# A planned decoder kernel: the DeltaNet inverse from 32-wide blocks, and two changes to the plan of its start

## The chip, the cores and the metric

One core of one Trainium2 chip runs the whole kernel. The metric is the device time in microseconds (us) of one execution, as the median of several runs. A profiled execution gives the trace; its span goes from the first instruction to the last.

## What is computed

Two decoder layers over 256 tokens of width 1024, float32. Each layer projects the normalised input once, runs three mixers side by side (gated DeltaNet, pooling, sparse attention with 64 keys a query), and merges them through gates and two projections. The part that matters here is DeltaNet, cut from the reference, with 4 heads and chunks of 64 tokens:

```
lmat = where(strict, (k_beta @ k^T) * decay, 0)      # 64 x 64, strictly lower
tmat = triangular_solve(eye + lmat, eye)             # unit lower triangular inverse
u    = tmat @ v_beta
w    = tmat @ (k_beta * exp(gc))
# per chunk: v_new = u - w @ state; o = q*exp(g) @ state + attn @ v_new; state = ...
```

The kernel works with chunks of 128 tokens, two of them, so it inverts eight 128 x 128 triangular matrices a layer (2 chunks, 4 heads).

## The kernel before

**The plan.** The code does not issue instructions in its own order. Each call on V, S, G, PE or DMA (VectorE, ScalarE, GpSimd, TensorE, and SyncE's DMA queue) is recorded as an operation with a modelled cost, and a planner (class Plan, lines 186 to 546) lays all of them out in time and then emits one fixed order for each engine. `cost` (line 222 on) holds the modelled costs; `lay_out` (line 353 on) is the list scheduler. TensorE takes operations by their place in the code plus a shift; the other engines take them by how late they may be, a due time that `deadlines` works back from the layout before. Six layouts are made and the best one by the model is kept. All instructions appear in the trace under line 544, where they are emitted, so the rows are read by tile names.

Buffers come from tags with a fixed number of slots, handed out in the order of the code. The mx banks (4 PSUM banks) may be handed out of order, but at most 6 places ahead of the first one not yet handed out (WM, line 60). Weights come in as raw (5 slots), are cast to a high part wh (mostly by ScalarE) and a low part wl (a VectorE subtraction of 128 x 1024), and each product with the 1024-wide input is made of three full-tile matmuls into a pj bank.

**Planned landing of DMAs.** Lines 513 to 515 add to a model of the transfers 600 ns and DELAY (line 52), 900 ns, for each DMA:

```python
dma_free = max(dma_free, at + (2500.0 if e == "POOL" else 1360.0)) + o.tail
o.end = dma_free + 600.0 + DELAY
```

The tail of a DMA is its bytes by 120, 262, 318 or 338 a ns, by the length of its rows (line 229). SyncE's queue starts at 730 ns in the model.

**Parameter rows.** Lines 643 to 648 load the conv weights, pool scales and output norm of both layers as 106 rows through GpSimd's DMA queue. Lines 697 to 704 turn them with one TensorE transpose into pt (128 x 2 x 53), copied out by ScalarE, and make hb, half of five columns, on VectorE. This stands before the first projection in the code, so its mx bank is the second one in the order (the first is that of the 40 warming matmuls). Its first user is the conv of the k columns (`wc` in the loop over qkv), far later.

**The inverse** (lines 1161 to 1189). Um holds the negated, scaled, strictly upper part of each matrix; uc holds its eight sets of 32 x 32 diagonal blocks side by side, 128 x 8 x 32. Before the change the two 16 x 16 halves of each diagonal block are inverted together, on VectorE, in 15 steps from r = 15 down to 1. A step has three VectorE operations on 8 x (16 - r) elements of each partition, each waiting for the one before it:

```python
V.stream_shuffle(xb[:, :, r:], x16[:, :, r:], [r] * 16 + [16 + r] * 16)
V.tensor_tensor(xb[:, :, r:], xb[:, :, r:], u16[:, :, r:r + 1].to_broadcast([128, 8, n]), op=ALU.mult)
V.tensor_tensor(x16[:, :, r:], x16[:, :, r:], xb[:, :, r:], op=ALU.add)
```

The halves are then put on the diagonal of xi, a VectorE transpose makes xt, and `joined` (line 1181) is called twice: 32 matmuls of 32 x 32 each (8 matrices, 4 row bands, the bands inside), um times xt and that times xi, which fills the off-diagonal quarter.

**From 32 to 128** (lines 1217 to 1256). For both chunks: p1, eight 32 x 32 matmuls; p2, four matmuls for tt's 32..64 rows (copied there by VectorE) and eight more; then p3, two times four matmuls of 64 x 64, with copies between them. The results Qm feed the DeltaNet recurrence (`four`), whose output o0, o1 is normalised, multiplied by the projected gate (`gated`), transposed into yah and yal, and multiplied into the branch projection, the third of the layer's three. The gate projections and the branch projections of the other two mixers do not depend on it.

A float32 matmul of TensorE shows as two records in the trace, one of a 4-byte split (fp32r) as one.

Of the kernel before, what the change touches and what calls it, by code (L numbers as in the profile page):

```python
# [9 lines left out]
F32 = mybir.dt.float32  # L10
# [20 lines left out]
for _n, _c in (("ident", 128), ("upper", 128), ("supper", 128), ("bd", 128),  # L31
               ("ncaus", 128), ("eye16", 16), ("cosa", 128), ("sina", 128), ("cosi", 64),
               ("sini", 64), ("rcount", 64), ("half", 2), ("strict", 128)):
    CST[_n] = (_w, _w + _c)
    _w += _c
# [10 lines left out]
SWITCH = 160.0  # L46
# [5 lines left out]
DELAY = 900.0  # L52
# [12 lines left out]
def constants():  # L65
# [13 lines left out]
    put("eye16", (p % 16) == np.arange(16)[None, :])  # L79
    put("half", np.concatenate([p % 32 < 16, p % 32 >= 16], axis=1))  # L80
# [105 lines left out]
class Plan:  # L186
# [35 lines left out]
    def cost(self, eng, call, args, kw):  # L222
# [8 lines left out]
        if eng == "PE":  # L231
            if call == "transpose":
                return 109.0, 170.0, False
            if args[1].ap.dtype == F32R:
                return (n / 2.4 + 13.3 if n > 100 else 60.0), 175.0, False
            m, k = args[1].shape[-1], args[1].shape[0]
            if k <= 32:
                return 12.0, 170.0, False
            if k <= 64:
                return 116.0, 170.0, False  # L240
            return 2 * (max(n, m) / 1.2 + 3), 170.0, False
# [111 lines left out]
    def lay_out(self):  # L353
# [98 lines left out]
        while len(order) < len(self.ops):  # L452
# [60 lines left out]
            if o.call == "dma_start":  # L513
                dma_free = max(dma_free, at + (2500.0 if e == "POOL" else 1360.0)) + o.tail
                o.end = dma_free + 600.0 + DELAY
# [33 lines left out]
def trunk(ctx: ExitStack, tc: tile.TileContext, x, norm_g, w_in, gate_b, conv_w, a_log, dt_bias, dn_onorm,  # L549
# [126 lines left out]
    um = make("um", [128, 8, 32])  # L676
    G.memset(um, 0.0)

# [16 lines left out]


    plan.shift = LATE + 300
    pp = bank("mx")
    PE.transpose(pp[:, :DEPTH * NPAR], rows[:DEPTH * NPAR, :], ident[:DEPTH * NPAR, :DEPTH * NPAR])
    pts = make("pt", [128, DEPTH, NPAR], F32)  # L700
    S.copy(pts, pp[:, :DEPTH * NPAR].rearrange("p (l n) -> p l n", l=DEPTH))
    hbs = make("hb", [128, DEPTH, 5], F32)
    V.tensor_scalar(hbs, pts[:, :, 48:53], 0.5, None, op0=ALU.mult)
    plan.shift = 0
# [17 lines left out]
    for l in range(DEPTH):  # L722
# [57 lines left out]
        pt, hb = pts[:, l], hbs[:, l]  # L780
# [139 lines left out]
        attend("q", QC)  # L920
        attend("v", VC)
# [238 lines left out]

        lower, upper_ = con("half")[:, 1:2], con("half")[:, 0:1]
        w16 = unit()
        u16, x16, xb = (w16[:, i * 128:(i + 1) * 128].rearrange("p (n j) -> p n j", n=8) for i in range(3))
        V.scalar_tensor_tensor(u16, uc[:, :, 16:], lower, uc[:, :, :16], op0=ALU.mult, op1=ALU.add)
        V.tensor_scalar(um[:, :, 16:], uc[:, :, 16:], upper_, None, op0=ALU.mult)
        V.tensor_copy(x16, con("eye16")[:, None, :].to_broadcast([128, 8, 16]))
        for r in range(15, 0, -1):
            n = 16 - r
            V.stream_shuffle(xb[:, :, r:], x16[:, :, r:], [r] * 16 + [16 + r] * 16)
            V.tensor_tensor(xb[:, :, r:], xb[:, :, r:], u16[:, :, r:r + 1].to_broadcast([128, 8, n]), op=ALU.mult)  # L1170
            V.tensor_tensor(x16[:, :, r:], x16[:, :, r:], xb[:, :, r:], op=ALU.add)

        xi = make("xi", [128, 8, 32], F32)
        w32 = unit()
        xt, z32 = (w32[:, i * 256:(i + 1) * 256].rearrange("p (n j) -> p n j", n=8) for i in range(2))
        V.tensor_scalar(xi[:, :, :16], x16, upper_, None, op0=ALU.mult)
        V.tensor_scalar(xi[:, :, 16:], x16, lower, None, op0=ALU.mult)
        V.transpose(xt, xi)
        bands = [slice(32 * b, 32 * b + 32) for b in range(4)]

        def joined(lhs, rhs):
            ps = bank("mx")[:, :256].rearrange("p (n j) -> p n j", n=8)
            for i in range(8):
                for bs in bands:
                    mm(ps[bs, i], lhs[bs, i], rhs[bs, i], True, True)
            return ps

        S.copy(z32, joined(um, xt))
        V.tensor_tensor(xi, joined(z32, xi), xi, op=ALU.add)

# [31 lines left out]
        pairs = [(a, slice(64 * a, 64 * a + 32), slice(64 * a + 32, 64 * a + 64)) for a in range(2)]  # L1222
        for c in range(2):
            c4 = slice(4 * c, 4 * c + 4)
            p1 = bank("mx")[:, :256].rearrange("p (a h j) -> p a h j", a=2, h=4)
            for a, lo32, hi32 in pairs:
                for h in range(4):
                    mm(p1[hi32, a, h], v4(Um[c])[lo32, h, hi32], tt[lo32, 4 * c + h, 0:32], True, True)
                (S.copy if a else V.tensor_copy)(y1[hi32, a, c4], p1[hi32, a])
        Qm = []  # L1230
        for c in range(2):
# [8 lines left out]
            p2 = bank("mx")[:, :384].rearrange("p (a h j) -> p a h j", a=3, h=4)  # L1240
            for h in range(4):
                mm(p2[32:64, 2, h], xi[32:64, 4 * c + h], y1[32:64, 0, 4 * c + h], True, True)
            V.tensor_copy(tt[32:64, c4, 0:32], p2[32:64, 2])
            for a, lo32, hi32 in pairs:
                for h in range(4):
                    mm(p2[lo32, a, h], y1[hi32, a, 4 * c + h], xi[hi32, 4 * c + h], True, True)
# [167 lines left out]
```

## Time and profile before

| | |
|---|---|
| median of 3 runs | 575.1 us (574.57 to 575.27) |
| profiled execution | 574.95 us, of which its span is 573.2 us |
| TensorE matmuls | 565.2 us busy, 99% of the span |
| TensorE weight loads | 497.9 us, beside the matmuls |
| VectorE | 482.7 us, 84% |
| ScalarE | 297.8 us, 52% |
| GpSimd | 40.3 us, 7% |
| granted TensorE clock | 1.00 in every stretch |
| DMA | 98.7 MB, 56.7% of 16 engines' span on the main queue |

How to read it: the busy share says which engine is full, not which one sets the end; for that the waits and the timeline are read. A busy time counts an instruction from its start to its end, and neighbours overlap: so what an operation takes out of a full engine's stream is the distance from one start to the next. In a timeline row the first number is the start and the second the time that the merged instructions cover, both in us. In a windows row each engine has its busy time in the stretch and the number of instructions, then come the granted clock, the DMA share and GB/s.

### The profile page before, as it was taken

How to read it: one execution, taken by the hardware profiler on the slowest of the kernel's cores; microseconds unless marked ns; L12 is line 12 of the kernel's file. 1: busy time of each engine (PE TensorE's matmuls, PEld its weight loads, DVE VectorE, ACT ScalarE, POOL GpSimd, SP SyncE). 2: the span in 40 equal slices, each digit the busy share in tenths (PEclk: the TensorE clock that was granted, in tenths of full speed). 3: DMA queues.
4: the chain of work that ended last, by engine and by line, in shares of the span. 5: the costliest groups of instructions: out<-in, count | busy, mean ns of one | idle time of the engine just before them, and what ended most of it. 6: DMA issues, size and time to landing. Idle time of an engine off the chain costs nothing. (4 is left out here: it accounts for less than half of the span.)

```text
span 573.2 us, 10046 instructions
## 1 busy us (share of the span) xinstructions
PE 565.2 (99%) x3750; PEld 497.9 (87%) x3750; DVE 482.7 (84%) x1026; ACT 297.8 (52%) x572; POOL 40.3 (7%) x49
## 2 busy tenths in 40 slices
PE   8999999999999999999999999999999999999997
PEld 7787999999888788888879889999998878888886
DVE  5995999999999767758599999999999966785672
ACT  6654646656563443644366645756454534444520
POOL 4210020000000101000011002000000020100000
PEclk9999999999999999999999999999999999999999
DMA  8795548283686543664646459457456643657411
GB/s 285 233 283 151 140 114 224 64 231 131 227 255 203 181 132 109 216 220 151 182 126 198 122 145 244 111 148 210 136 186 205 203 157 89 200 168 238 161 38 73
DMA packets 89792, 98.70 MB, mean 172 GB/s; under 512 B 5616, under 2 KB 58656, under 8 KB 89744
## 3 DMA queue, kind: packets, MB, share of 16 engines
q1 hardware_dynamic: 89184, 97.47, 56.7%
q0 software_dynamic: 560, 0.60, 0.6%
q8 instruction: 29, 0.48, 0.3%
q14 instruction: 19, 0.16, 0.1%
HBM read 97.00 MB, written 1.05 MB: 171 GB/s over the span
## 5 line engine op out<-in xcount | busy, mean ns | idle before, releaser
L544 ACT CAST wh<-raw 128x1024 fp32r<-128x1024 f32 (+2 forms) x167 | 175.0, 1052 | 158.5 <-PE pj L544 116.0
L544 DVE TENSOR_TENSOR wl<-raw,wh 128x1024 fp32r<-128x1024 f32 (+1 forms) x174 | 209.6, 1217 | 18.0 <-PE pj L544 10.7
L544 PE MATMUL pj<-wh,hh 128*128 128x512 f32 (+1 forms) x352 | 101.3, 389 | 0.4 <-ACT hh L544 0.4
L544 PE MATMUL pj<-wl,hh 128*128 128x512 f32 (+1 forms) x352 | 101.2, 387 | 0.0
L544 PE MATMUL pj<-wh,hl 128*128 128x512 f32 (+1 forms) x352 | 99.7, 386 | 0.4 <-DVE hl L544 0.3
L544 PEld LDWEIGHTS pj<-wh,hl 128*128 128x128 f32 x352 | 65.1, 188 | 14.1 <-DVE hl L544 1.9
L544 PEld LDWEIGHTS pj<-wh,hh 128*128 128x128 f32 x352 | 64.5, 188 | 12.9 <-ACT hh L544 1.3
L544 PEld LDWEIGHTS pj<-wl,hh 128*128 128x128 f32 x352 | 64.8, 188 | 12.0
L544 PE MATMUL pj<-hh,wh 128*128 128x256 f32 x384 | 56.3, 285 | 0.0
L544 PE MATMUL pj<-hh,wl 128*128 128x256 f32 x384 | 54.9, 284 | 0.0
L544 PE MATMUL pj<-hl,wh 128*128 128x256 f32 x384 | 54.6, 284 | 0.0
L544 PE MATMUL pj<-wh,y 128*128 128x512 f32 (+1 forms) x208 | 51.6, 383 | 0.0
L544 PEld LDWEIGHTS pj<-hh,wh 128*128 128x128 f32 x384 | 50.4, 191 | 0.2
L544 PEld LDWEIGHTS pj<-hh,wl 128*128 128x128 f32 x384 | 49.8, 192 | 0.0
L544 PEld LDWEIGHTS pj<-hl,wh 128*128 128x128 f32 x384 | 49.7, 192 | 0.0
L544 PEld LDWEIGHTS pj<-wh,y 128*128 128x128 f32 x208 | 38.5, 188 | 7.5
L544 PE MATMUL mx<-wh,y 128*128 128x512 f32 (+1 forms) x128 | 38.4, 380 | 0.0
L544 PEld LDWEIGHTS mx<-u,u 128*128 128x128 f32 (+2 forms) x336 | 31.3, 164 | 3.2 <-issue 1.4
L544 PE MATMUL mx<-u,u 128*128 128x128 f32 (+2 forms) x336 | 32.9, 249 | 0.0
L544 DVE SCALAR_TENSOR_TENSOR u<-pj,pt,u 128x255 f32<-128x255 f32 (+2 forms) x72 | 29.3, 470 | 0.0
L544 PE MATMUL pj<-wl,y 128*128 128x512 f32 (+1 forms) x104 | 29.2, 387 | 0.0
L544 PEld LDWEIGHTS mx<-wh,y 128*128 128x128 f32 x128 | 23.3, 188 | 4.4 <-DVE y L544 0.2
(210 smaller groups left out, 662.5 us busy)
## 6 DMA issues: line engine op xcount, KB each, us to landing
raw<-in_w_in_dram SPq DMA_DIRECT2D x128, 512.0 KB, 4.0
raw<-in_w_branch_dram SPq DMA_DIRECT2D x24, 512.0 KB, 4.0
raw<-in_w_out_dram SPq DMA_DIRECT2D x16, 512.0 KB, 3.2
tg<-in_gate_b_dram SPq DMA_DIRECT2D x12, 256.0 KB, 4.2
raw<-in_w_in_dram SPq DMA_DIRECT2D x4, 486.0 KB, 6.5
x_sb<-in_x_dram SPq DMA_DIRECT2D x2, 512.0 KB, 4.4
out_dram<-x_sb SPq DMA_DIRECT2D x3, 256.0 KB, 2.0
raw<-in_w_in_dram SPq DMA_DIRECT2D x2, 324.0 KB, 5.1
```

The source lines that it names most:

```text
L544: getattr(self.real[o.eng], o.call)(*[put(a) for a in o.args], **{k: put(v) for k, v in o.kw.items()})
```

## The change

The inverse of a 32 x 32 diagonal block is made in one piece: 31 steps on VectorE from r = 31 to 1, on 8 x (32 - r) elements each; the 16-wide halves, um, the two joining products and the constants for them go. p1 and p2 have their loops over the two 64-row halves inside the loop over heads; the four extra matmuls of p2 go, and VectorE transposes p2's first result instead of copying the extra one. The parameter rows are turned after the attention's q heads of layer 0 instead of before the first projection. In the planner, the 900 ns are added only to DMAs issued after 10 us, a switch between small and full tiles costs 103 ns instead of 160, and matmuls of up to 32 and 64 rows cost 21 and 134 ns instead of 12 and 116. The diff, with the constants' renaming left out:

```diff
-SWITCH = 160.0
+SWITCH = 103.0
-DELAY = 900.0
+DELAY, CALM = 900.0, 10000.0
...
             if k <= 32:
-                return 12.0, 170.0, False
+                return 21.0, 170.0, False
             if k <= 64:
-                return 116.0, 170.0, False
+                return 134.0, 170.0, False
...
-                o.end = dma_free + 600.0 + DELAY
+                o.end = dma_free + 600.0 + (DELAY if at > CALM else 0.0)
...
-    um = make("um", [128, 8, 32])
-    G.memset(um, 0.0)
...
-    plan.shift = LATE + 300
-    pp = bank("mx")
-    PE.transpose(pp[:, :DEPTH * NPAR], rows[:DEPTH * NPAR, :], ident[:DEPTH * NPAR, :DEPTH * NPAR])
-    pts = make("pt", [128, DEPTH, NPAR], F32)
-    S.copy(pts, pp[:, :DEPTH * NPAR].rearrange("p (l n) -> p l n", l=DEPTH))
-    hbs = make("hb", [128, DEPTH, 5], F32)
-    V.tensor_scalar(hbs, pts[:, :, 48:53], 0.5, None, op0=ALU.mult)
-    plan.shift = 0
...
         attend("q", QC)
+        if l == 0:
+
+            pp = bank("mx")
...
+        pt, hb = pts[:, l], hbs[:, l]
         attend("v", VC)
...
-        V.scalar_tensor_tensor(u16, uc[:, :, 16:], lower, uc[:, :, :16], op0=ALU.mult, op1=ALU.add)
-        V.tensor_scalar(um[:, :, 16:], uc[:, :, 16:], upper_, None, op0=ALU.mult)
-        V.tensor_copy(x16, con("eye16")[:, None, :].to_broadcast([128, 8, 16]))
-        for r in range(15, 0, -1):
...
-        V.tensor_scalar(xi[:, :, :16], x16, upper_, None, op0=ALU.mult)
-        V.tensor_scalar(xi[:, :, 16:], x16, lower, None, op0=ALU.mult)
-        V.transpose(xt, xi)
...
-        S.copy(z32, joined(um, xt))
-        V.tensor_tensor(xi, joined(z32, xi), xi, op=ALU.add)
+        xb = make("xb", [128, 8, 32], F32)
+        V.tensor_copy(xi, con("eye32")[:, None, :].to_broadcast([128, 8, 32]))
+        for r in range(31, 0, -1):
+            n = 32 - r
+            V.stream_shuffle(xb[:, :, r:], xi[:, :, r:], [r] * 32)
+            V.tensor_tensor(xb[:, :, r:], xb[:, :, r:], uc[:, :, r:r + 1].to_broadcast([128, 8, n]), op=ALU.mult)
+            V.tensor_tensor(xi[:, :, r:], xi[:, :, r:], xb[:, :, r:], op=ALU.add)
...
+            for h in range(4):
+                for a, lo32, hi32 in pairs:
+                    mm(p1[hi32, a, h], v4(Um[c])[lo32, h, hi32], tt[lo32, 4 * c + h, 0:32], True, True)
             for a, lo32, hi32 in pairs:
-                for h in range(4):
-                    mm(p1[hi32, a, h], v4(Um[c])[lo32, h, hi32], tt[lo32, 4 * c + h, 0:32], True, True)
                 (S.copy if a else V.tensor_copy)(y1[hi32, a, c4], p1[hi32, a])
...
             for h in range(4):
-                mm(p2[32:64, 2, h], xi[32:64, 4 * c + h], y1[32:64, 0, 4 * c + h], True, True)
-            V.tensor_copy(tt[32:64, c4, 0:32], p2[32:64, 2])
+                for a, lo32, hi32 in pairs:
+                    mm(p2[lo32, a, h], y1[hi32, a, 4 * c + h], xi[hi32, 4 * c + h], True, True)
+            V.transpose(tt[32:64, c4, 0:32], p2[0:32, 0])
             for a, lo32, hi32 in pairs:
-                for h in range(4):
-                    mm(p2[lo32, a, h], y1[hi32, a, 4 * c + h], xi[hi32, 4 * c + h], True, True)
                 S.copy(q4[lo32, :, hi32], p2[lo32, a])
```

## Rows read from the trace of the kernel before

**Rows 1.** The page's busy times: us, share of the span, instructions.

```profile
PE 565.2 (99%) x3750; PEld 497.9 (87%) x3750; DVE 482.7 (84%) x1026; ACT 297.8 (52%) x572; POOL 40.3 (7%) x49
```

**Rows 2.** TensorE's waits: for whom, total us, times, longest us.

```profile
PE mx L544 <- DVE big L544: 1.6, 4, 0.9
...
PE mx L544 <- ACT kiT L544: 0.9, 1, 0.9
```

**Rows 3.** Timeline of TensorE, 189 to 202 us, around layer 0's inverse.

```profile
189.15 1.07 PE L544 MATMUL pj<-wl,hh 128*128 128x512 f32 x4
190.15 0.75 PE L544 MATMUL mx<-u,um 32*32 32x32 f32 x64
190.83 1.20 PE L544 MATMUL pj<-wh,hh 128*128 128x512 f32 x4
191.87 1.08 PE L544 MATMUL pj<-wh,hl 128*128 128x512 f32 x4
...
197.19 0.89 PE L544 MATMUL mx<-u,u 32*32 32x32 f32 x32
198.01 0.50 PE L544 MATMUL pj<-wl,hh 128*128 128x512 f32 x1
...
200.73 0.34 PE L544 MATMUL mx<-u,xi 32*32 32x32 f32 x5
...
201.86 0.73 PE L544 MATMUL pj<-wl,hh 128*128 128x512 f32 x2
```

**Rows 4.** Timeline of VectorE: the inverse and its end in both layers.

```profile
163.32 0.19 DVE L544 STREAM_SHUFFLE u<-u 128x8 f32<-128x8 f32 x1
...
176.04 0.22 DVE L544 STREAM_SHUFFLE u<-u 128x64 f32<-128x64 f32 x1
...
176.82 0.26 DVE L544 STREAM_SHUFFLE u<-u 128x72 f32<-128x72 f32 x1
...
184.22 0.29 DVE L544 STREAM_SHUFFLE u<-u 128x104 f32<-128x104 f32 x1
...
185.16 0.29 DVE L544 STREAM_SHUFFLE u<-u 128x112 f32<-128x112 f32 x1
...
188.57 0.47 DVE L544 TENSOR_SCALAR xi<-u,cs 128x128 f32<-128x128 f32 x2
...
194.36 0.42 DVE L544 TENSOR_TENSOR xi<-mx,xi 128x256 f32<-128x256 f32 x1 [2.12 <-PE mx L544]
...
238.38 0.75 DVE L544 SCALAR_TENSOR_TENSOR y<-mx,hb,y 128x512 fp32r<-128x512 f32 x1 [0.62 <-ACT y L544]
...
459.52 0.42 DVE L544 TENSOR_TENSOR xi<-mx,xi 128x256 f32<-128x256 f32 x1 [1.82 <-PE mx L544]
```

**Rows 5.** Groups of instructions of VectorE: busy us, mean ns of one, idle before.

```profile
L544 DVE STREAM_TRANSPOSE u<-xi 128x256 f32<-128x256 f32 x4 | 1.7, 436 | 0.0
```

**Rows 6.** Busy time of each engine in three stretches.

```profile
40.00:60.00 20.00, 19.14 (x97) 15.98 (x96) 14.22 (x32) 11.73 (x28) 0.00 (x0) 1.00 0.59 162
60.00:160.00 100.00, 99.72 (x772) 96.13 (x772) 99.81 (x228) 59.63 (x120) 5.82 (x5) 1.00 0.57 165
189.00:216.00 27.00, 27.00 (x350) 22.09 (x349) 18.09 (x31) 12.10 (x25) 3.65 (x2) 1.00 0.53 162
```

**Rows 7.** Timeline of TensorE: the first matmuls of DeltaNet's branch projection, both layers.

```profile
255.85 1.98 PE L544 MATMUL pj<-wh,y 128*128 128x512 f32 x8
...
534.62 1.98 PE L544 MATMUL pj<-wh,y 128*128 128x512 f32 x8
```

**Rows 8.** The parameter rows' transpose in the timeline, and the first use of its result.

```profile
53.34 0.25 PE L544 MATMUL mx<-cs,rows 106*128 106x106 f32 x1
...
L544 ACT ACTIVATE u<-pj,pt x24: 452/468/498, 97.0 to 393.5; 128x256 f32<-128x256 f32 x24
```

**Rows 9.** Timeline of VectorE at the start: first readers of x and of a weight.

```profile
4.13 0.69 DVE L544 SCALAR_TENSOR_TENSOR f<-x_sb 128x512 f32<-128x512 f32 x1 [3.27 <-DMA x_sb<-in_x_dram]
...
8.69 0.70 DVE L544 CAST wh<-raw 128x1024 fp32r<-128x1024 f32 x1 [0.23 <-DMA raw<-in_w_in_dram]
```

More of the change, by code (lines that the diff above doesn't have):

```diff
@@ L31 @@
 for _n, _c in (("ident", 128), ("upper", 128), ("supper", 128), ("bd", 128),
-               ("ncaus", 128), ("eye16", 16), ("cosa", 128), ("sina", 128), ("cosi", 64),
-               ("sini", 64), ("rcount", 64), ("half", 2), ("strict", 128)):
+               ("ncaus", 128), ("eye32", 32), ("cosa", 128), ("sina", 128), ("cosi", 64),
+               ("sini", 64), ("rcount", 64), ("strict", 128)):
     CST[_n] = (_w, _w + _c)
@@ L78, in constants @@
     put("ncaus", np.where(j > p, FILL, 0.0))
-    put("eye16", (p % 16) == np.arange(16)[None, :])
-    put("half", np.concatenate([p % 32 < 16, p % 32 >= 16], axis=1))
+    put("eye32", (p % 32) == np.arange(32)[None, :])
     for n, dim in (("a", 128), ("i", 64)):
@@ L920, in trunk @@
         attend("q", QC)
+        if l == 0:
+            pp = bank("mx")
+            PE.transpose(pp[:, :DEPTH * NPAR], rows[:DEPTH * NPAR, :], ident[:DEPTH * NPAR, :DEPTH * NPAR])
+            pts = make("pt", [128, DEPTH, NPAR], F32)
+            S.copy(pts, pp[:, :DEPTH * NPAR].rearrange("p (l n) -> p l n", l=DEPTH))
+            hbs = make("hb", [128, DEPTH, 5], F32)
+            V.tensor_scalar(hbs, pts[:, :, 48:53], 0.5, None, op0=ALU.mult)
+        pt, hb = pts[:, l], hbs[:, l]
         attend("v", VC)
@@ L1157, in trunk @@
         V.tensor_scalar(c1, eg[:, 4:8], -1.0, None, op0=ALU.mult)
-        lower, upper_ = con("half")[:, 1:2], con("half")[:, 0:1]
-        w16 = unit()
-        u16, x16, xb = (w16[:, i * 128:(i + 1) * 128].rearrange("p (n j) -> p n j", n=8) for i in range(3))
-        V.scalar_tensor_tensor(u16, uc[:, :, 16:], lower, uc[:, :, :16], op0=ALU.mult, op1=ALU.add)
-        V.tensor_scalar(um[:, :, 16:], uc[:, :, 16:], upper_, None, op0=ALU.mult)
-        V.tensor_copy(x16, con("eye16")[:, None, :].to_broadcast([128, 8, 16]))
-        for r in range(15, 0, -1):
[L1168 to L1171, printed above, removed]
-        xi = make("xi", [128, 8, 32], F32)
-        w32 = unit()
-        xt, z32 = (w32[:, i * 256:(i + 1) * 256].rearrange("p (n j) -> p n j", n=8) for i in range(2))
-        V.tensor_scalar(xi[:, :, :16], x16, upper_, None, op0=ALU.mult)
-        V.tensor_scalar(xi[:, :, 16:], x16, lower, None, op0=ALU.mult)
-        V.transpose(xt, xi)
[L1179 to L1186, printed above, removed]
-        S.copy(z32, joined(um, xt))
-        V.tensor_tensor(xi, joined(z32, xi), xi, op=ALU.add)
+        xi = make("xi", [128, 8, 32], F32)
+        xb = make("xb", [128, 8, 32], F32)
[5 more added lines that the diff above has]
+            V.tensor_tensor(xi[:, :, r:], xi[:, :, r:], xb[:, :, r:], op=ALU.add)
         for c in range(2):
@@ L1239, in trunk @@
                             .to_broadcast([128, 4, 4, 32]), op=ALU.mult)
-            p2 = bank("mx")[:, :384].rearrange("p (a h j) -> p a h j", a=3, h=4)
+            p2 = bank("mx")[:, :256].rearrange("p (a h j) -> p a h j", a=2, h=4)
             for h in range(4):
-                mm(p2[32:64, 2, h], xi[32:64, 4 * c + h], y1[32:64, 0, 4 * c + h], True, True)
-            V.tensor_copy(tt[32:64, c4, 0:32], p2[32:64, 2])
+                for a, lo32, hi32 in pairs:
+                    mm(p2[lo32, a, h], y1[hi32, a, 4 * c + h], xi[hi32, 4 * c + h], True, True)
+            V.transpose(tt[32:64, c4, 0:32], p2[0:32, 0])
             for a, lo32, hi32 in pairs:
-                for h in range(4):
-                    mm(p2[lo32, a, h], y1[hi32, a, 4 * c + h], xi[hi32, 4 * c + h], True, True)
                 S.copy(q4[lo32, :, hi32], p2[lo32, a])
```

1 line of the change is left out of this document (removed).

## The prediction

> **What bounds the kernel now.** I read the busy shares first: TensorE's matmuls cover 565.2 of 573.2 us, VectorE's work 482.7 [rows 1]. So the end is set by how much TensorE has to do and by the little that it waits. Next the waits of TensorE: the two longest kinds are four waits for big, 1.6 us together, and one for kiT, 0.9 us [rows 2]; three more kinds are shorter. Then TensorE's timeline where the DeltaNet inverse is made, to see what each small group takes out of the stream [rows 3]; then VectorE's timeline, to see what the inverse takes there [rows 4]; last, the room between the inverse and the matmuls that cannot start without it [rows 6, 7]. What to see: an operation that leaves TensorE is worth its place in the stream, and VectorE work is free only as long as its result comes before TensorE has used up everything else.
>
> **Removed from TensorE: the two joining products.** Each is 32 matmuls, 64 records. Four full-tile matmuls take 0.91 us in the stream, so after the four that start at 189.15 the next was due at 190.06; it came at 190.83, and those four took 1.04 instead of 0.91 [rows 3]. One group costs 0.77 + 0.13 = 0.90 us, its entry and exit included; the other three groups of the two layers look alike in the timeline. Four times 0.90 is **3.6 us**.
>
> **The small products that stay.** The first group (p1) has 32 records in 0.82 us, 25.6 ns each; the second (p2) 48 records in 1.13 us, 23.5 ns each [rows 3]. In both, most neighbours use the same 32x32 tile of the array. In the joining product each neighbour uses another of four tiles: 64 records in 0.68 us, 10.6 ns each. The change alternates two tiles in p1 and p2, and p2 loses its four extra matmuls of each chunk (48 records become 32). Bounds for 32 records: 0.34 us at 10.6 ns, 0.82 us at 25.6 ns. I take half of the one-tile rate, since only two tiles alternate: 0.41 us each. p1 saves 0.41 (0 to 0.48), p2 0.72 (0.31 to 0.79), 1.13 a layer, **2.3 us** for both (0.6 to 2.5). The 64-wide products of p3 keep their order and price.
>
> TensorE in all: 3.6 + 2.3 = **5.9 us less** (4.2 to 6.1).
>
> **The transpose by VectorE** takes the place of a VectorE copy of the same columns. The nearest row, a transpose of twice the columns, is 0.44 us [rows 5]. There are four, in the same place of the inverse's tail as the copies, beside full-tile matmuls on TensorE that hide them; between nothing and 4 x 0.44 = 1.8 us of VectorE, and I take nothing, as a copy goes for each. Without that cover the tail is at most 0.44 us longer for each chunk.
>
> **Added to VectorE: 31 steps for 15.** A step is a shuffle and two tensor_tensor, one after the other, and its width is 8 elements for each column reached. Dense, the 64-wide step took 0.78 us from start to start (176.04 to 176.82), the 104-wide one 0.94 (184.22 to 185.16) [rows 4], so 4 ns an element on 0.52 us. 31 steps of a mean width of 128 are 31 x 1.04 = 32.1 us, the 15 steps of mean width 64 were 15 x 0.78 = 11.7. The two halves' preparation, the scalings, one transpose and the last addition go, six operations of 0.2 to 0.45 us, about 2 us. Net **18.4 us more VectorE a layer**, 37 in all: 482.7 becomes about 520 us, 91% of the span. What goes with it is the wait for the two joining products: from the last 16-wide step to the finished inverse at 194.8 about 6 us [rows 4].
>
> **Does it fit?** In layer 0 the inverse runs from 163.3 to 194.8 [rows 4], its result reaches the gated output at 239.1 (238.38 + 0.75) [rows 4], and the branch matmuls that need it start at 255.85 [rows 7]. That is 16.7 us of room, 13.8 with 2.9 us less to run ahead of it. VectorE is idle for 27 - 18.1 = 8.9 us between 189 and 216 and for 20 - 14.2 = 5.8 us between 40 and 60; from 60 to 160 it is full [rows 6]. The work that it has in hand beside the inverse makes the low weight parts that TensorE's next matmuls need and empties their banks, so it can't all step back. The inverse alone could be ready at 163.3 + 32.1 = 195.4, no later than now; at its old share it would be far later (the second rival). Layer 1 has 75 us from its inverse (459.5) to its branch matmuls (534.62), layer 0 only 61.5 [rows 4, 7]. I take it that the planner, which ranks VectorE's operations by how late they may be, gives the longer chain the larger share and finds most of the 18.4 us in the idle time of 40 to 60 and behind 189. TensorE then waits a little more than now. For that I add **1.2 us**: with VectorE full over long stretches, all that TensorE waited for VectorE's big was 1.6 us [rows 2], and I take three quarters as much again; bounds 0 and the second rival.
>
> **The parameter rows.** One TensorE transpose, one ScalarE copy and one VectorE scaling move from before the projections to behind the q heads. Their DMAs keep their place on GpSimd's queue, and nothing moves on SyncE's queue. The transpose ran at 53.34, and the first user of its result starts at 97.0 [rows 8], so a later place delays nobody as long as it stays before that; its costs stay the same. But its bank is the second in the order of the mx banks, of which only six may be handed out ahead: the k transposes and the index work queued behind it ran right after 53.34, and there TensorE waited 0.9 us for kiT [rows 2]. Moved, that queue drains earlier, beside the projections; what is late next there is the q heads' work, which then has the transpose in its neighbourhood. I take **0.6 us** of the 0.9 (0 to 0.9), and the 5.8 us of VectorE above become usable.
>
> **First transfers.** The planner's landing time of early DMAs drops by 0.9 us, and with it the order on the engines; no DMA is added. Worked from the planner's own constants, the first half of x was expected at 5.14 and is now expected at 4.24; its first reader started at 4.13 [rows 9]. The first weights were expected at about 8.6 and are now at 7.7; their first reader started at 8.69 [rows 9]. So the new plan is right for x and about 1 us early for weights. Most of TensorE's waits for big lie in the first 10 us: bounds -1.6 [rows 2] and +1.0; I take **0**, as the two transfers point opposite ways. The planner's other constants (a switch of tile size at 103, small matmuls at 21 and 134) change no instruction by themselves.
>
> **Sum.** The profiled execution took 574.95 us (its span 573.2), 0.15 below the median of the runs. 574.95 - 5.9 - 0.6 + 0 + 1.2 = 569.65, so 569.8 on the medians.
>
> **First rival: the new order saves nothing.** The p1 row itself speaks for it: 25.6 ns a record, and p2, where two operand pairs alternate in part, is hardly faster. Against it stands the joining product's 10.6 ns. At 25.6 ns only the joining products and the 16 records a layer of p2 are saved, 4.2 us: 574.95 - 4.2 - 0.6 + 1.2, **571.5** on the medians. The Trainium skill, page "TensorE: Matmul & The Clock Gate", section "Wait — 56ns, not 53.3ns?", has such a rule: start to start never drops below about 25 ns, however few the columns. By that rule the order gains nothing; p1's row agrees with it, the joining product's row does not, and the row decides.
>
> **Second rival, slower: the inverse comes too late in layer 0.** In the old chain 15 steps took 25.2 us from 163.32 to the last one's end, 1.68 a step, because VectorE put other work between them [rows 4]. At that pace, with 0.26 for the width, 31 steps are 60 us: ready at 223.5 instead of 194.8, 28.7 later against 13.8 of room. The branch matmuls of layer 0 would stand still for 14.9 us: 574.95 - 6.5 + 14.9, **583.5** on the medians. Layer 1, with 13.6 us more room, would just hold. It decides against the change from 6.5 us of standing still, when the inverse of layer 0 ends after about 215. For it: VectorE is full from 60 on. Against it: the old chain had no need to hurry with 16.7 us of room, and the idle time of [rows 6] covers most of the extra. The Trainium skill speaks for this rival: "VectorE: DVE Perf Modes", section "Rules for kernel authors", advises to keep the number of chained VectorE operations low. The rows agree that small operations are dear: a shuffle of 8 elements takes 0.19 us, one of 112 takes 0.29 [rows 4].
>
> **Third rival: the transfers are planned too early.** The weights' reader of [rows 9] speaks for it: engines that take their work in a fixed order then stand at a weight that is not there, 1.0 us once: **570.8**.
>
> **How the numbers follow.** My forecast has 0.60, the first rival 0.12, the third 0.11, the second 0.17. The first three are all faster than 575.1; of their 0.83 I move 0.06 to no change, for a stall of 4 to 6 us that eats the gain. About 0.2%, 1.15 us, is what a measurement of this kernel can tell from no change. Faster 0.77, same 0.06, slower 0.17. The low end has all savings at their best, no new wait and 1.0 of the start's 1.6: 574.95 - 6.1 - 0.9 - 1.0 = 566.95, about 567.0; the high end is where new waits have eaten all, 575.0, which leaves out the second rival.
>
> **What would show it.** Right: records um and the first joining groups gone, p1 and p2 near 0.4 us each, TensorE busy near 559 us, VectorE near 90%, the wait for kiT gone, no TensorE wait over 1 us past 60 us (its longest for big was 0.9). The first rival shows as p1 at 0.8 us. The second shows as a wait of several us ahead of layer 0's branch matmuls, on VectorE, and perhaps a lower granted clock after it. The third shows as TensorE or ScalarE waiting for raw before 20 us. A TensorE busy time that did not fall, or waits spread over the whole span, would make my reading wrong.

## The result, and the profile after

The changed kernel takes **568.56 us** (median of 4 runs, 568.06 to 569.16) against 575.12 us of the kernel before on the same chip (4 runs, 574.57 to 575.27): a ratio of 0.9888, 95% interval 0.9871 to 0.9905. That is 6.6 us faster; 569.8 was predicted, with a range of 567.0 to 575.0. Here and below the times are medians and the ratios are of means; one execution of 618.75 us of the kernel before and one of 3192.59 us of the first experiment, which is the one that was profiled there, are left out. The profiled execution of the changed kernel took 569.16 us, its span 567.1 us, and the granted clock was 1.00 in every stretch.

The page's busy times and the waits of TensorE in the changed kernel (for whom, us in total, times, longest us), which answer to [rows 1, 2]:

```profile
PE 560.5 (99%) x3462; PEld 495.0 (87%) x3462; DVE 507.3 (89%) x1140; ACT 301.0 (53%) x575; POOL 30.8 (5%) x45
```

```profile
PE mx L543 <- POOL wh L543: 1.1, 1, 1.1
PE mx L543 <- DVE big L543: 0.8, 3, 0.3
PE mx L543 <- DVE u L543: 0.5, 1, 0.5
PE pj L543 <- ACT hh L543: 0.5, 1, 0.5
PE pj L543 <- DVE hl L543: 0.5, 1, 0.5
```

The budget of the span is best made from 10 us on. Up to there TensorE runs warming matmuls in the time that it has to wait, so that busy time says little; the first projection matmul starts at 10.41 us before and at 10.40 after. The first 10 us of the kernel before, in the columns of [rows 6]:

```profile
0.00:10.00 10.00, 7.81 (x50) 7.24 (x50) 3.78 (x12) 5.25 (x14) 3.65 (x13) 1.00 0.80 268
```

TensorE is busy for 7.81 us of the first 10 before and for 8.58 after, which leaves 565.2 - 7.8 = 557.4 and 560.5 - 8.6 = 551.9 us: **5.5 us less busy**. The rest of the span after 10 us is 563.2 - 557.4 = 5.8 us before and 557.1 - 551.9 = 5.2 after: **0.6 us less idle**. Together they are the 6.1 us by which the span is shorter. The records of TensorE went down by 3750 - 3462 = 288: four joining groups of 64 and two times the 16 records that p2 lost. The wait for kiT is gone; that for big lost its longest one, 0.86 us at 9.99, which was part of the start. One wait for u is new: p1 stands 0.52 us for the end of the inverse.

TensorE's timeline around layer 0's inverse, and from the last transposes of the branch output to the matmuls that need them; it answers to [rows 3, 7]:

```profile
221.15 0.69 PE L543 MATMUL mx<-u,u 32*32 32x32 f32 x32 [0.52 <-DVE u L543]
221.78 1.21 PE L543 MATMUL pj<-wl,hh 128*128 128x512 f32 x4
...
224.54 0.69 PE L543 MATMUL mx<-xi,u 32*32 32x32 f32 x32
225.16 0.51 PE L543 MATMUL pj<-wh,hl 128*128 128x512 f32 x1
...
250.10 0.60 PE L543 MATMUL mx<-cs,u 128*128 128x128 f32 x4
252.60 1.98 PE L543 MATMUL pj<-wh,y 128*128 128x512 f32 x8
```

p1 takes 221.78 - 221.15 = 0.63 us out of the stream, p2 0.62; they took 0.82 and 1.13 [rows 3]. The last two rows show how little room is left: the last transposes of the output that the branch matmuls multiply start at 250.10, the branch matmuls at 252.60, 2.5 us later. Before, the transposes started at 237.02 and the branch matmuls at 255.85 [rows 7], 18.8 us later. Timeline of TensorE in the kernel before:

```profile
237.02 0.60 PE L544 MATMUL mx<-cs,u 128*128 128x128 f32 x4
```

VectorE's timeline in layer 0: two early steps of the inverse, then the last operation of the last step; it answers to [rows 4]:

```profile
154.86 0.17 DVE L543 TENSOR_TENSOR xb<-xb,uc 128x16 f32<-128x16 f32 x1
154.94 0.28 DVE L543 TENSOR_TENSOR tsq<-cs,qn 128x128 f32<-128x128 f32 x1
...
159.73 0.19 DVE L543 TENSOR_TENSOR xb<-xb,uc 128x32 f32<-128x32 f32 x1
159.96 0.19 DVE L543 TENSOR_TENSOR xi<-xi,xb 128x32 f32<-128x32 f32 x1
...
219.21 0.40 DVE L543 TENSOR_TENSOR xi<-xi,xb 128x248 f32<-128x248 f32 x1
```

The inverse's first operation on uc starts at 153.9 us, about 10 us earlier than before, and its last one ends at 219.21 + 0.40 = 219.6 instead of 194.8: some 66 us for 31 steps, where the old chain with its two joining products had 31.5. The first four rows show what a small operation takes out of a full VectorE. At 154.86 an independent operation follows, and it starts 0.08 us later; at 159.73 the next operation needs the result, and it starts 0.23 us later. The wide operations at the end save about as much: at 219.21 the next one, which is independent, starts 0.32 us later, while with a dependent one behind it a 248-wide operation took 0.45 us (228.49 to 228.94 in the kernel with the new inverse alone, below). So a chain woven among other work takes some 0.12 to 0.15 us less of the stream for each link that is woven.

The busy time of each engine in three stretches of the changed kernel, with the columns of [rows 6]; after the stretch and its length come TensorE's matmuls, its weight loads and VectorE:

```profile
0.00:10.00 10.00, 8.58 (x49) 7.88 (x49) 2.44 (x9) 4.42 (x8) 3.08 (x12) 1.00 0.80 269
...
40.00:60.00 20.00, 20.00 (x97) 16.47 (x97) 20.00 (x63) 12.73 (x31) 0.00 (x0) 1.00 0.44 116
...
192.00:221.00 29.00, 28.63 (x127) 23.37 (x125) 28.55 (x65) 12.70 (x14) 0.00 (x0) 1.00 0.61 179
```

The first row is the one used in the budget above. Both of VectorE's gaps that the prediction wanted to fill are full: between 40 and 60 us it is busy 20.00 us instead of 14.22, and between 192 and 221 it is busy 28.55 of 29.00.

### The profile page after: what moved, and what is told of

The parts are those of the page before. It is cut to its first block, busy times and chain, and to the rows that moved or that the text cites. A ratio compares the mean times of both kernels' runs of the same rounds, so it can differ in the third digit from the quotient of the medians.

```text
span 567.1 us, 9577 instructions
## 1 busy us (share of the span) xinstructions
PE 560.5 (99%) x3462; PEld 495.0 (87%) x3462; DVE 507.3 (89%) x1140; ACT 301.0 (53%) x575; POOL 30.8 (5%) x45
## 5 line engine op out<-in xcount | busy, mean ns | idle before, releaser
L543 ACT CAST wh<-raw 128x1024 fp32r<-128x1024 f32 (+1 forms) x168 | 175.6, 1050 | 137.9 <-PE pj L543 107.4
L543 DVE TENSOR_TENSOR wl<-raw,wh 128x1024 fp32r<-128x1024 f32 (+1 forms) x174 | 209.3, 1212 | 10.6 <-issue 2.9
L543 PE MATMUL pj<-wh,hl 128*128 128x512 f32 (+1 forms) x352 | 101.5, 388 | 0.5 <-DVE hl L543 0.5
L543 PE MATMUL pj<-hh,wh 128*128 128x256 f32 x384 | 55.1, 285 | 0.0
```

Source lines behind the costliest of these rows:

```text
L543: getattr(self.real[o.eng], o.call)(*[put(a) for a in o.args], **{k: put(v) for k, v in o.kw.items()})
```

## The experiments

**The question.** TensorE lost about 5 us of work, but VectorE got 24.6 us more, and layer 0's inverse ends 25 us later. The theory: the gain is TensorE's, and it can be kept because turning the parameter rows late frees VectorE's idle time before 60 us. The rivals: the rows have nothing to do with it, or it is the planned start that gives the time. The first five kernels split the change into its parts. Every ratio below is to the kernel before on the same chip.

**Without the new inverse.** The changed kernel with the old inverse, its joining products and the old p1 and p2; the rows late and the new planner constants stay.

```diff
-        V.tensor_copy(xi, con("eye32")[:, None, :].to_broadcast([128, 8, 32]))
-        for r in range(31, 0, -1):
...
+        for r in range(15, 0, -1):
...
+        S.copy(z32, joined(um, xt))
+        V.tensor_tensor(xi, joined(z32, xi), xi, op=ALU.add)
```

> The changed kernel with the old inverse put back: 16-wide halves, the two joining products, and p1 and p2 with their old loops and the four extra matmuls. What is left of the change is the planner's constants, the landing times of early transfers and the later transpose of the parameter rows. Theory (the gain is TensorE work taken out of a full stream): the joining products cost 3.6 us again and p1 and p2 together about 1.4 us, so about 573.5 us, within 1 us. Rival (the gain comes from the start and the parameter rows): 569 to 570 us, p1 and p2 back at 0.8 and 1.1 us a layer all the same.

Measured: 573.56 us, ratio 0.9978 (0.9969 to 0.9987). Against 0.9888 of the whole change, the inverse with its products is worth 0.90% of 575 us, 5.2 us, in a kernel that has the rest.

**The new inverse alone.** The kernel before with the 31 steps, the new p1 and p2 and VectorE's transpose; the rows and the planner as before.

```diff
+        V.tensor_copy(xi, con("eye32")[:, None, :].to_broadcast([128, 8, 32]))
+        for r in range(31, 0, -1):
...
-            V.tensor_copy(tt[32:64, c4, 0:32], p2[32:64, 2])
+            V.transpose(tt[32:64, c4, 0:32], p2[0:32, 0])
```

> The kernel before with the new inverse and the new p1 and p2 alone; the planner's constants, the landing times and the place of the parameter rows stay old. Theory: 5.0 us less TensorE work than before, so about 570 us. If the VectorE time that the moved parameter rows set free between 40 and 60 us is needed, layer 0's inverse ends some 6 us later than in the changed kernel (219.6), the room of 2.5 us ahead of the branch matmuls is gone, and the time is 572 to 574 us, with a wait of TensorE ahead of p1 of 2 us or more. Rival (gain from the start and the rows): 574 to 575 us with TensorE's busy time not lower.

Measured: 575.6 us, ratio 1.0007 (0.9998 to 1.0016). The same edit that is worth 5.2 us above is worth nothing here, and the time is above the 572 to 574 us that were expected for this case; TensorE does not wait ahead of p1, as was expected, but ahead of the branch matmuls. Where it went is in three views of this kernel: VectorE's timeline at the inverse's end, TensorE's timeline from there to the branch matmuls, and the windows before and after it.

```profile
228.94 0.42 DVE L543 TENSOR_TENSOR xi<-xi,xb 128x248 f32<-128x248 f32 x1
```

```profile
252.06 1.13 PE L543 MATMUL mx<-u,u 128*128 128x128 f32 x8 [0.17 <-DVE u L543]
...
253.77 0.66 PE L543 MATMUL mx<-cs,u 128*128 128x128 f32 x4 [0.58 <-DVE u L543]
...
256.25 2.40 PE L543 MATMUL pj<-wh,y 128*128 128x512 f32 x4 [1.82 <-ACT y L543]
```

```profile
40.00:60.00 20.00, 19.14 (x100) 16.10 (x99) 14.33 (x33) 11.34 (x27) 0.00 (x0) 1.00 0.59 160
...
252.00:257.00 5.00, 2.54 (x14) 1.89 (x14) 5.00 (x9) 3.00 (x11) 0.20 (x1) 0.92 0.00 0
257.00:262.00 5.00, 5.00 (x20) 3.66 (x19) 2.71 (x5) 0.69 (x1) 0.80 (x1) 0.74 0.33 105
```

The inverse ends at 228.94 + 0.42 = 229.4, 9.8 us later than in the changed kernel. By 252 us TensorE has run out of other work; it is busy for 2.54 us of the next 5, with three waits of 2.57 us in sum, and then the granted clock falls: 0.92 and 0.74 in the two windows are means over 2.4 GHz and the lower level, 1.2 GHz. Against full speed this is (1 - 0.92) x 5 + (1 - 0.74) x 5 = 1.7 us lost. With the waits it makes 4.3 us, and the first projection matmul starts 0.45 us later (10.86). The lower clock is not in every execution: one of the eleven had a granted clock of 1.00, and took 574.16 us; nine had 0.997, and took 575.4 us in the mean. Between 40 and 60 us VectorE is idle for 5.7 us as before, since the rows still stand early. This is the mechanism of the prediction's second rival.

**The rows early again.** The changed kernel with the transpose of the parameter rows at its old place ahead of the first projection.

```diff
+    plan.shift = LATE + 300
+    pp = bank("mx")
+    PE.transpose(pp[:, :DEPTH * NPAR], rows[:DEPTH * NPAR, :], ident[:DEPTH * NPAR, :DEPTH * NPAR])
...
-        if l == 0:
-
-            pp = bank("mx")
```

> The changed kernel with the parameter rows transposed at the old place, before the first projection. Theory: the k transposes and the index work queue behind it again, TensorE waits about 0.9 us for kiT near 55 us, and VectorE idles 4 to 6 us between 40 and 60; the inverse of layer 0 then ends later by up to 6 us and TensorE waits for it: 569.2 to 572 us. Rival (the place of the rows changes nothing, because the wait only moves): 568.6 us, within 0.4.

Measured: 573.05 us, ratio 0.9978 (0.9966 to 0.9989). Moving one transpose back costs 0.90%, 5.2 us in the mean, more than was expected (572 us at most). The seven executions differ by the clock: four at a granted clock of 1.00 took 572.84 to 573.05 us, three at 0.997 took 574.20 to 574.79. So at full clock the move costs some 4.4 us, and the lower clock, where it comes, about 1.5 more. The waits of TensorE in the profiled execution, which is one of the four, and VectorE's share between 40 and 60 us and the inverse's last operation:

```profile
PE mx L543 <- DVE big L543: 1.8, 4, 0.7
PE mx L543 <- DVE u L543: 1.6, 1, 1.6
...
PE mx L543 <- ACT kiT L543: 0.9, 1, 0.9
```

```profile
40.00:60.00 20.00, 19.14 (x100) 16.11 (x100) 14.28 (x30) 11.35 (x27) 0.00 (x0) 1.00 0.60 161
```

```profile
225.23 0.42 DVE L543 TENSOR_TENSOR xi<-xi,xb 128x248 f32<-128x248 f32 x1
```

The wait for kiT is back, VectorE's idle time before 60 us is back, and the inverse ends at 225.7 instead of 219.6. The new wait of 1.6 us for u stands among the branch matmuls, at 257.55; one of 0.35 us for y stands ahead of it and one of 0.67 us for big behind it.

**The rows late alone.** The kernel before with nothing but this move.

```diff
         attend("q", QC)
+        if l == 0:
+
+            pp = bank("mx")
...
+        pt, hb = pts[:, l], hbs[:, l]
```

> The kernel before with the parameter rows transposed behind the q heads and nothing else changed. Theory (the place of the rows frees VectorE time, which is worth something only where VectorE's result is awaited): the wait for kiT near 55 us goes, VectorE is full between 40 and 60 us, and the time falls by that wait alone, 0.6 to 1.0 us: 574.1 to 574.5. Rival (the place of the rows is worth 4.5 us by itself, as putting it back into the changed kernel cost that much): 570 to 571 us.

Measured: 572.85 us, ratio 0.9965 (0.9953 to 0.9977), a span of 571.1 us. Neither expectation held: the move is worth 2.0 us by itself, more than the kiT wait and less than the 5.2 us that it is worth beside the new inverse. The waits of TensorE and the window from 40 to 60:

```profile
PE mx L544 <- POOL wh L544: 1.1, 1, 1.1
PE pj L544 <- ACT wh L544: 0.4, 1, 0.4
PE mx L544 <- DVE big L544: 0.4, 2, 0.2
```

```profile
40.00:60.00 20.00, 20.00 (x100) 16.76 (x100) 20.00 (x60) 13.15 (x31) 0.00 (x0) 1.00 0.45 122
```

The wait for kiT is gone, and so is one of 0.44 us for hh at 20.74; one of 0.4 us for a weight is new. Counted from 10 us on as above (8.73 us busy before that, and the first projection matmul at 10.40 here too), TensorE is idle for 561.1 - 556.5 = 4.6 us instead of 5.8, and busy for 556.5 instead of 557.4: 1.2 us of waiting and 0.9 us of a stream that does the same work in another order. The branch matmuls of layer 0 start at 254.01 instead of 255.85 and those of layer 1 at 532.85 instead of 534.62 [rows 7]: 1.8 us are gained before 254 and only kept afterwards. The first of the index products (kiT with qiT) in TensorE's timeline, first this kernel's row, then that of the kernel before:

```profile
34.12 1.05 PE L544 MATMUL mx<-kiT,qiT 128*128 128x128 f32 x8
...
55.23 0.74 PE L544 MATMUL mx<-kiT,qiT 128*128 128x128 f32 x4 [0.86 <-ACT kiT L544]
```

With the rows early, the index products run just behind the rows' transpose at 53.34 [rows 8]; with the rows late they run 21 us earlier, and VectorE's first top-k operation moves from 66.41 to 49.74, into the idle time. That it is the order of the banks that held them back is read from the code and fits these rows; no run changes that order alone.

**Both, on the planner of before.** The kernel before with the rows late and the new inverse, but with the old constants and the old landing times.

```diff
         attend("q", QC)
+        if l == 0:
+
+            pp = bank("mx")
...
-        for r in range(15, 0, -1):
...
+        for r in range(31, 0, -1):
```

> The kernel before with two parts of the change alone: the parameter rows transposed behind the q heads, and the new inverse with the new p1 and p2. The planner's constants and the landing times stay old. Theory (the later rows make the room that the longer inverse needs, the landing times and constants are worth nothing): the 2.0 us of the rows by themselves and the 5.0 us of TensorE work add up, 575 - 7 = 568 us, within 0.7, as in the run with all transfers delayed (567.93). Rival (the constants matter for the layout): 569.5 us or more.

Measured: 568.01 us, ratio 0.9882 (0.9866 to 0.9899), not to be told from the whole change. So the two program edits make all of the gain, and the planner's constants none that can be measured. Here the effect of the inverse is at its cleanest, since this kernel and the one above differ in nothing else: the first branch matmuls move from 254.01 to 251.44 in layer 0 and from 532.85 to 527.72 in layer 1, 2.6 us for each layer, 5.1 together, although the first projection matmul starts 0.25 us later (10.65). The first two rows are of the kernel with the rows late alone, the last two of this one:

```profile
254.01 1.98 PE L544 MATMUL pj<-wh,y 128*128 128x512 f32 x8
...
532.85 1.98 PE L544 MATMUL pj<-wh,y 128*128 128x512 f32 x8
...
251.44 1.98 PE L543 MATMUL pj<-wh,y 128*128 128x512 f32 x8
...
527.72 1.98 PE L543 MATMUL pj<-wh,y 128*128 128x512 f32 x8
```

TensorE's busy time after 10 us falls from 556.5 to 559.8 - 8.3 = 551.5, 4.9 us. The inverse ends at 216.9:

```profile
216.45 0.41 DVE L543 TENSOR_TENSOR xi<-xi,xb 128x248 f32<-128x248 f32 x1
```

The four corners side by side, ratios to the kernel before:

| | old inverse | new inverse |
|---|---|---|
| rows early | 1 | 1.0007 (old planner constants), 0.9978 (new) |
| rows late | 0.9965 (old), 0.9978 (new) | 0.9882 (old), 0.9888 (new) |

**Is it the load on VectorE, or the place in the queue?** The kernel with the new inverse alone, and four of layer 0's eight rounds of the top-k selection left out, which takes VectorE work out ahead of the inverse.

```diff
-            for r in range(8):
+            for r in range(8 if l else 4):
```

> The kernel before with the new inverse alone (rows early), and in layer 0 only 4 of the 8 rounds that pick the 64 keys: the selection is left half done there. Each round is about 1.55 us of VectorE over both halves of the tokens, so 6.2 us of VectorE go, about what lies idle between 40 and 60 us with the rows early; the rows keep their place and the wait for kiT stays. Theory (what counts is how much VectorE has to do before the inverse ends): layer 0's inverse ends at about 223 instead of 229.4, the stall ahead of the branch matmuls and the half-clock spell behind it go, and the time is 570 to 571.5 us instead of 575.6. Rival (it is the place in the queue, not the load): 575 us still, with the inverse's end past 228.

Measured: 569.57 us, ratio 0.9912 (0.9897 to 0.9926), 0.95% or 5.5 us less than with all eight rounds.

```profile
40.00:60.00 20.00, 19.14 (x99) 16.06 (x98) 14.32 (x33) 11.35 (x27) 0.00 (x0) 1.00 0.61 160
```

```profile
221.62 0.42 DVE L543 TENSOR_TENSOR xi<-xi,xb 128x248 f32<-128x248 f32 x1
```

```profile
255.69 1.89 PE L543 MATMUL pj<-wh,y 128*128 128x512 f32 x7 [0.54 <-ACT y L543]
```

The rows still stand early, the kiT wait is still 0.9 us and the gap between 40 and 60 us is still 5.7 us wide. But the inverse ends at 222.0 instead of 229.4, the stall at the branch matmuls has shrunk to one wait of 0.54 us for y among them, and the granted clock stays at 1.00. TensorE has the same 3462 records in both kernels, and the time came back: what the early rows cost is VectorE time ahead of the inverse.

**A slower inverse.** The changed kernel with the shuffle of each step done twice.

```diff
             V.stream_shuffle(xb[:, :, r:], xi[:, :, r:], [r] * 32)
+            V.stream_shuffle(xb[:, :, r:], xi[:, :, r:], [r] * 32)
```

> The changed kernel with each step's shuffle done twice: 31 more VectorE operations of 0.19 to 0.44 us a layer, some 9 us, on the inverse's own chain. Theory (2.5 us of room are left in layer 0 and about 7 in layer 1): TensorE stands still for 4 to 8 us ahead of layer 0's branch matmuls and for little in layer 1, the granted clock drops to half for some us behind a long stall, and the time is 573 to 579 us. Rival (VectorE's other work gives way, as it did in the change): 569 to 570 us.

Measured: 585.21 us, ratio 1.0177 (1.0163 to 1.0191), more than the 573 to 579 us expected.

```profile
PE 568.7 (97%) x3462; PEld 499.9 (86%) x3462; DVE 522.4 (90%) x1268; ACT 299.9 (51%) x572; POOL 31.2 (5%) x44
```

```profile
50.00:60.00 10.00, 7.67 (x42) 6.61 (x41) 10.00 (x29) 0.59 (x1) 2.01 (x2) 0.83 0.15 38
255.00:270.00 15.00, 11.64 (x51) 8.80 (x50) 11.56 (x17) 6.57 (x16) 1.01 (x1) 0.89 0.26 86
538.00:552.00 14.00, 11.71 (x54) 8.86 (x53) 11.11 (x17) 7.04 (x16) 1.25 (x2) 0.88 0.24 76
```

15 us more of VectorE cost 16.4 us of span. The inverse of layer 0 ends at 231.3, and TensorE stands before the branch matmuls of both layers, each time with a lower clock behind it (0.89 and 0.88). The third stall, between 50 and 60 us, was in nobody's expectation: the planner laid the start out in another order as well. So this run shows that no room is left, but not a clean price of one step.

**The order of the small products.** The changed kernel with the loops over the halves outside again in p1 and p2.

```diff
-            for h in range(4):
-                for a, lo32, hi32 in pairs:
+            for a, lo32, hi32 in pairs:
+                for h in range(4):
```

> The changed kernel with only the loops of p1 and p2 turned back, the halves outside and the heads inside; VectorE's transpose and the smaller p2 stay. Theory (two alternating tiles save a little): p1 and p2 take 0.8 us each instead of 0.63, 0.35 us a layer more, 0.7 us in all: about 569.3 us. If alternating were worth the half rate of the forecast, 1.6 us more: 570.2. If the order saved nothing: 568.6 and the groups at 0.63 us still.

Measured: 568.94 us, ratio 0.9895 (0.9879 to 0.9911); the median is 0.4 us above the changed kernel's, and the intervals overlap. The trace tells the two apart. Timeline of TensorE:

```profile
220.26 0.89 PE L543 MATMUL mx<-u,u 32*32 32x32 f32 x32
221.08 1.20 PE L543 MATMUL pj<-wl,hh 128*128 128x512 f32 x4
...
223.80 0.89 PE L543 MATMUL mx<-xi,u 32*32 32x32 f32 x32
224.62 0.50 PE L543 MATMUL pj<-wh,hl 128*128 128x512 f32 x1
```

In the old order both groups take 0.82 us, 25.6 ns a record; alternating two tiles they take 0.63 and 0.62 us, 19.6 ns. The order is worth 0.2 us a group, 0.8 us in all.

**The planned landing.** The changed kernel with the 900 ns on every DMA, as before the change, and one with them left out only of DMAs before 2.3 us, which covers x but not the first weights.

```diff
-DELAY, CALM = 900.0, 10000.0
+DELAY, CALM = 900.0, 0.0
...
-DELAY, CALM = 900.0, 10000.0
+DELAY, CALM = 900.0, 2300.0
```

> The changed kernel with the 900 ns added to the landing of every DMA again. Theory (the two early transfers point opposite ways): the start's order comes back, with a wait for x's second half and the first weight cast on VectorE, and the time stays within 0.5 us of 568.6. If the earlier landing of x was worth its 0.9 us: 569.5. If planning the weights too early cost 1 us: 567.6.

> The changed kernel with the 900 ns added to DMAs issued after 2.3 us instead of 10 us: x and the constants are planned early, the weights as in the kernel before. Theory: the first cast goes to VectorE (0.7 us) instead of ScalarE (1.05 us), ScalarE's first hh copies are not behind a cast that waits for its transfer, and the first projection matmul starts at 9.5 to 10.1 us instead of 10.40: 0.3 to 0.9 us faster than the changed kernel, 567.7 to 568.3. Rival (the start is set by the transfers themselves): 568.6, within 0.3.

Measured: 567.93 us, 0.9884 (0.9871 to 0.9898), and 568.91 us, 0.9898 (0.9884 to 0.9911). Neither can be told from the changed kernel. The first lies between the two values that its expectation tells apart, so it leaves open whether the earlier landing costs some tenths of a us. In the second the first projection matmul was to start at 9.5 to 10.1 us; it started at 11.70, and no gain came.

**A still earlier inverse.** The kernel with rows and inverse on the planner of before, with ScalarE in place of VectorE for the copies into uc.

```diff
-                V.tensor_copy(uc[bs, c4, :], v4(z)[bs, :, bs])
+                S.copy(uc[bs, c4, :], v4(z)[bs, :, bs])
```

> The same two parts as in the run with rows and inverse, and the sixteen small copies into uc may go to ScalarE, as the planner chooses; 3.5 us of VectorE lie in them. Theory: TensorE has almost no waits left to remove, so the same time as with rows and inverse, within 0.4 us, with layer 0's inverse ending 1 to 3 us earlier. Rival (VectorE still limits): 0.5 to 1 us faster, 567.3 or less.

Measured: 567.59 us, ratio 0.9877 (0.9863 to 0.9892), the lowest median of all, but not to be told from 568.01 without this edit. The inverse ends at 212.46 + 0.41 = 212.9, 4 us earlier, and 14 of the 16 copies ran on ScalarE, but nothing that can be measured follows from it: once TensorE does not wait for the inverse, an earlier one is worth nothing.

## Why the prediction was right, and where its terms were not

**What bounds the kernel** held: of the 6.1 us by which the span fell, 5.5 are TensorE's busy time, and it is still busy for 99% of what remains. That the sum came within 1.2 us is in part luck, since three of its terms were wrong by 0.7 to 1.4 us and not all the same way, and the second rival was close: leaving the rows at their place is enough to bring its mechanism about.

**TensorE, predicted 5.9 us, measured about 5.0.** The joining products' 3.6 us [rows 3] stand. The mis-sized term is p1 and p2: predicted 0.41 us each, measured 0.63 and 0.62, so 1.4 us saved instead of 2.3. The assumption that two alternating tiles take half of the one-tile rate was wrong; they take three quarters of it. The move of the branch matmuls in the pair of kernels that differ in the inverse alone, 2.6 us a layer, and the 4.9 us of busy time between them confirm 3.6 + 1.4 = 5.0.

**The first rival (the order saves nothing, 571.5)** fell: 25.6 ns became 19.6, in a run where only the order differs. The rule of the Trainium skill behind it, in "TensorE: Matmul & The Clock Gate", section "Wait — 56ns, not 53.3ns?", of about 25 ns from start to start, agrees with the rows for neighbours on one tile (25.6 ns), and not with those on two (19.6) or four (10.6) [rows 3].

**VectorE, predicted 37 us more, measured 24.6.** The mis-sized step is the price of a dense chain, 0.78 to 0.94 us a step [rows 4]. The planner wove other work between part of the links, and each of those takes 0.12 to 0.15 us less. Added up from start to start in the traces, the 31 steps take some 26.5 us a layer where the prediction had 32.1, and the old 15 some 9.7 where it had 11.7; that is 7 of the 12 us. The rest is in part that busy time leaves out the gaps of a dependent chain, which the forecast counted; it was not split further. The VectorE transpose out of PSUM costs nothing, as predicted: it takes 285 ns, as did the copy that it replaces.

```profile
L543 DVE STREAM_TRANSPOSE u<-mx 32x128 f32<-32x128 f32 x4 | 1.0, 285 | 0.1
```

**Does it fit?** It does, as forecast, in the idle time of 40 to 60 us and behind 189 [rows 6]. But the margin was misjudged. The prediction let the second rival decide from an inverse that ends after about 215; it ended at 219.6 and cost 0.52 us. The chain from the inverse to the branch matmuls had slack in it that the prediction counted as needed, since the old kernel had no cause to hurry: from the inverse's end to the last transposes it was 237.02 - 194.8 = 42 us before and 250.10 - 219.6 = 30.5 us after. The ends that were tried, in four kernels, bracket the limit: 219.6 goes with one wait of 0.52 us, 222.0 with one of 0.54, 225.7 with two of 1.9 us together, and 229.4 with 2.6 us of waits and in most executions the lower clock behind them.

**The parameter rows, predicted 0.6 us, measured 2.0 alone.** This is the term that was right in its mechanism and too small by a factor of three: besides the wait for kiT, 0.9 us go because the same matmuls take less time in the new order, of which the prediction had no term. And the sentence that named 5.8 us of VectorE as becoming usable had no number in the sum, though it carries the forecast: without the move the new inverse is worth nothing on the old planner constants, with it 5 us. The cover of the inverse should have been named as conditional on this move.

**New waits, predicted 1.2 us:** one of 0.52 us came for the inverse, and TensorE's idle time after 10 us fell by 0.6. The 0.7 us too many, with the 1.4 us too little for the rows, outweigh the 0.9 us too much for p1 and p2; by that the result lies 1.2 us below the forecast. **The start, predicted 0:** TensorE's first projection matmul starts at 10.40 instead of 10.41, and the two runs on the landing times differ from the changed kernel by less than can be told.

**The second rival (583.5)** did not come to pass, but its mechanism is real; the new inverse alone shows it. Its price there, about 5 us and not 14.9, eats the saving of 5 us, and 575.6 is left. The advice of the Trainium skill in "VectorE: DVE Perf Modes", section "Rules for kernel authors", to keep the number of chained VectorE operations low, fits that kernel and the doubled shuffle (15 us more of VectorE, 16.4 us of span), and not the whole change, whose chain doubled its steps and cost TensorE one wait of 0.52 us.

**The third rival (570.8)** is there in its mechanism, and worth less than these runs can tell from nothing. The first cast of weights stands 0.51 us for its transfer, the first writing of hh is queued behind it, and so TensorE's first projection matmul waits 0.51 us for hh. But before the change it stood 0.86 us for big ahead of the same matmul, and it starts at the same time. Timeline of ScalarE in the changed kernel:

```profile
9.03 1.05 ACT L543 CAST wh<-raw 128x1024 fp32r<-128x1024 f32 x1 [0.51 <-DMA raw<-in_w_in_dram]
9.99 0.62 ACT L543 ACTIVATE hh<-mx,g 128x128 fp32r<-128x128 f32 x2
```

**Open:** why the new inverse with early rows takes 2.5 us less on the new planner constants (573.05) than on the old ones (575.6). Part of it is the clock, which fell in ten of eleven executions on the old ones and in three of seven on the new. At the same granted clock about 1 us is left: 574.16 against 572.84 to 573.05 us at 1.00, 575.4 against 574.4 in the mean at 0.997. There the inverse ends 3.7 us earlier, which was not traced to one of the constants.

## What to carry to other kernels

Work that leaves the full engine is worth its place in the stream only if what replaces it elsewhere is ready in time: look for the idle time that the replacement needs, and for what keeps that idle time from being used (here, as far as code and rows show, one early buffer in a queue that is handed out in order). Two edits can then be worth nothing and 2 us apart and 7 us together, so a part should be tried with and without the other before it is dropped. A dependent chain of small VectorE operations should be priced by the stream that it takes when woven, and its end by the slack of everything behind it.

## What the runs showed of the hardware that was not expected

In the profiled execution of the kernel with the new inverse alone, TensorE's granted clock fell after a stretch in which the engine was busy 2.54 of 5.00 us with no single wait over 1.82 us; in that of the kernel with the rows early it stayed at 1.00, with waits of 0.35, 1.56 and 0.67 us around the same place. One fixed order of instructions can do both: ten of eleven executions of the first kernel and three of seven of the second had a mean granted clock of 0.997 or less, the others 1.00, and at 0.997 they took 1.3 and 1.5 us longer. Small float32 matmuls of 32 x 32 took 25.6 ns a record on one tile, 19.6 on two tiles in turn and 10.6 on four. VectorE transposed 32 x 128 elements out of PSUM into another quarter of the partitions in 285 ns, the price of a plain copy.
